# A decoder block on Trainium2: head 1's queries and keys as a Strassen pair, another order in a pair's second half, group norm's scaling on ScalarE

## The chip, the cores and the metric

The kernel runs on one core of one Trainium2 chip. The metric is the device time of one execution in microseconds (us). TensorE (PE) multiplies, VectorE (DVE) and ScalarE (ACT) work on tiles, GpSimd (POOL) does little arithmetic here and issues the accumulating DMAs, SyncE (SP) issues the plain ones. About 1% is what a measurement of this kernel can tell from no change.

## The reference

One layer of a hybrid decoder, batch 1, 512 tokens, 1024 channels, everything in float32: a chunkwise retention (4 heads, keys of 128, values of 256) beside a sliding-window attention with sinks (8 query heads, 2 key heads), then an MLP with squared ReLU.

```python
h = rmsnorm(x, pre_mix_norm)
q_r, k_r, v_r, g_r, q_s, k_s, v_s, gate_r, gate_s = split(h @ w_in)
ret = retention_chunkwise(q_r, k_r, v_r)         # (B, T, 4, 256)
    # per chunk of 128: o = (q k^T * decay) v + (q * decay) state
    # mu, var over the 256 channels of a head:  (o - mu) * rsqrt(var + EPS)
y_r = (silu(g_r) * ret) @ w_ret_out
y_s = swa_gqa_sinks(q_s, k_s, v_s, sinks) @ w_swa_out
merged = sigmoid(gate_r) * y_r + sigmoid(gate_s) * y_s
x = x + rmsnorm(merged @ w_out, post_mix_norm)
u = square(relu(rmsnorm(x, pre_mlp_norm) @ w_up))
x = x + rmsnorm(u @ w_down, post_mlp_norm)
```

The change touches the projection of `q_r` and `k_r` (how they are multiplied, not what) and the last line of the retention, the group norm of each head.

## The kernel before

Every float32 product is done as three matmuls of a reduced float32 type: an operand is split into a high part (a cast on ScalarE, line 144) and the rest (a subtraction on VectorE, line 145), and `mm3` multiplies high by high (L188), high by rest (L189, L190). So each weight tile that comes in as `raw` needs a cast to `whi` and a subtraction to `wlo` before TensorE can use it.

Many of the products are made with a Strassen scheme of one level (Winograd's form): instead of the eight products of half-size blocks there are seven. Of the tokens it needs the blocks `11`, `21`, `22` and four sums `t1` to `t4`, made once (`hB`; `hT` are the blocks and `hsum` the sums). Of the weights it needs the blocks `11`, `12`, `22` and four sums `s1` to `s4`. `sums_into` loads two blocks into a tile `rs` by a plain DMA on SP (L220) and adds two more by an accumulating DMA on POOL (L221), which has to wait until the plain one has landed; that gives `s1` and `s3`. `wino_weights` then works in this order: it splits `raw` into `11` and `12`, splits `rs` into `s1` and `s3` (`whi`, `wlo`), adds to `rs` in place twice on VectorE (L241, L242), which gives `s2` and `s4`, splits these into `p24`, and last splits `22` into `p22`.

The retention works head by head. In the loop over heads, head h computes its decayed keys, its scores, its state products (`ret_st`) and its values (`ret_v`), and between these stand the products that make the queries and keys of head h + 1. The constant `DIRECT` says how many heads are made by plain blocks. It is 2, so heads 0 and 1 are made by `ret_block` (24 matmuls of 128x512 each for queries and for keys, tile `pblk`), heads 2 and 3 by `ret_pair`: seven products of 12 matmuls of 128x256 (tiles `rpair`), four in `first()`, three in `second()`. One PSUM tile, `chain`, accumulates several of them, and ScalarE copies it out after each (L745 and others in `first()`, L753 in `second()`): the next product on `chain` can't start before that copy is done.

The sums of the weights of head 2 are loaded while the window heads are still at work, into a part of the tile `retn` that is not yet needed; those of head 3 are loaded into the pool `wx`, which is opened in head 0's turn after `bctx` has been closed. The place of that pool is free only when what lay there is done with, so its first load waits for the last matmul (`pso`) of the last window head, `swa_values(3)`. Behind it on SP come, in this order, the loads of `w_g` (the gate of the retention, `wide_sums`) and of the first sums of `w_gate`.

The order on each engine is the order of the program as a scheduler has arranged it; every engine works its list strictly in order and waits at its own instructions. The tile pools give a place again when the last reader has finished, and a load into it waits for that on its queue.

Group norm is done per head at the end of `ret_values`: `bns` and `mv` hold mean and variance, `rms` the variance plus a constant (VectorE), `rr` its power −1/2 (POOL), and four instructions on VectorE (L601), one for each block of 128 tokens, subtract the mean and multiply by `rr` from PSUM into `retn`. `retn` is read only after the stage.

Of the kernel before, what the change touches and what calls it, by code (L numbers as in the profile page):

```python
# [10 lines left out]
F32 = mybir.dt.float32  # L11
F32R = mybir.dt.float32r
AF = mybir.ActivationFunctionType
# [3 lines left out]
P = 128  # L17
# [17 lines left out]
WARM = 7  # L35
LEFT_AHEAD = 300
T2_DMA = 4
DIRECT = 2

C_QR, C_KR, C_VR, C_GR, C_QS, C_KS, C_GATE_R = (0, 512, 1024, 2048, 3072, 3584, 3840)  # L40

# [62 lines left out]
def block_kernel(ctx, tc, x, xT, pre_mix, w_in, w_qk, w_v, w_g, w_gate, w_ret, w_swa, w_out, sinks, post_mix,  # L104
# [119 lines left out]
    def wino_load(w):  # L224

        raw = raw_tile([P, 3, 4, P])
        nc.sync.dma_start(raw[:, 0:2], w[:, 2:4])
        nc.sync.dma_start(raw[:, 2], w[:, 0])
        return raw

    def wino_weights(wx, rs, raw, px=None):

        a11, a12, a22 = raw[:, 0], raw[:, 1], raw[:, 2]

        def two(t, i, j):
            return {i: tuple(a[:, 0] for a in t), j: tuple(a[:, 1] for a in t)}

        w = two(parts(raw[:, :2], [P, 2, 4, P]), "11", "12")
        yield w
        w.update(two(parts(rs, [P, 2, 4, P]), "s1", "s3"))  # L240
        nc.vector.tensor_tensor(rs[:, 0], rs[:, 0], a11, op=ALU.add)  # L241
        last["sum"] = nc.vector.tensor_tensor(rs[:, 1], rs[:, 0], a12, op=ALU.add)  # L242
        yield w
        p24 = [(px or wx).tile([P, 2, 4, P], F32R, name=f"p24{i}") for i in range(2)]
        split(p24[0], p24[1], rs)
        w.update(two(p24, "s2", "s4"))
        yield w
        with tc.issue_after(last["hi"].ins):
            p22 = [wx.tile([P, 4, P], F32R, name=f"p22{i}") for i in range(2)]
            split(p22[0], p22[1], a22)  # L250
        w["22"] = tuple(p22)
        yield w

    def wino_first(steps):
        return list(steps)[-1]
# [167 lines left out]
    nc.sync.dma_start(sink_sb, sinks.to_broadcast([P, SWA_HEADS]))  # L423


    def swa_queries(ps):

        qs = dpool.tile([P, SEQ], F32, name="qs", bufs=4)
        nc.vector.scalar_tensor_tensor(qs, ps, SWA_DH**-0.5, R, op0=ALU.mult, op1=ALU.mult)
        return qs  # L430

# [142 lines left out]
    def ret_values(q, pt, states, v, h):  # L574
        mv = rpool.tile([P, NT, 2], F32, name="mv")
        retn = retns[h // 2][:, :, (h % 2) * RET_DV : (h % 2 + 1) * RET_DV]
        pss = []
        for ip in range(2):
            ps = bank([P, 2, RET_DV], "ret_v")
            for i in range(2):  # L580
                c = 2 * ip + i
                mm3(
                    ps[:, i, :], tuple(a[:, c, :] for a in pt), tuple(a[:, c, :] for a in v),
                    True, c == 0,
                )
                if c:
                    mm3(
                        ps[:, i, :], tuple(a[:, (c - 1) * P : c * P] for a in q),
                        states[c - 1], False, True,
                    )  # L590
            for i in range(2):
                st = rpool.tile([P, nc.vector.BN_STATS_DIM], F32, name="bns")
                nc.vector.bn_stats(st, ps[:, i, :])
                nc.vector.bn_aggr(mv[:, 2 * ip + i, :], st)
            pss.append(ps)
        ms = rpool.tile([P, NT], F32, name="rms")
        r = rpool.tile([P, NT], F32, name="rr")
        nc.vector.tensor_scalar(ms, mv[:, :, 1], chunk_sb[:, 1, h : h + 1], None, op0=ALU.add)
        nc.gpsimd.tensor_tensor(r, ms, mhalf, op=ALU.pow)
        for ib in range(NT):  # L600
            nc.vector.tensor_scalar(  # L601
                retn[:, ib, :], pss[ib // 2][:, ib % 2, :], mv[:, ib, 0:1], r[:, ib : ib + 1],
                op0=ALU.subtract, op1=ALU.mult,
            )


# [78 lines left out]

    def load_qk(h):
        if h >= DIRECT:
            return wino_first(wino_weights(wx, qk_sums[h], wino_load(w_qk[h - DIRECT])))
        return load_feature_blocks(w_in, (C_QR + h * RET_DK, C_KR + h * RET_DK))


    qs = [swa_queries(qs_ps[0])]
    kk2 = dpool.tile([P, SWA_KV, NT, 2, SWA_DH], F32, name="kk2", tag="s")
    ksT = dpool.tile([P, SWA_KV, SEQ], F32, name="ksT", bufs=1)
    for g in range(SWA_KV):
        for i in range(2):
            nc.gpsimd.tensor_copy(kk2[:, g, :, i, :], kv[:, :, g * SWA_DH : (g + 1) * SWA_DH])
    qs.append(swa_queries(qs_ps[1]))
    wq = load_feature_pair(w_in, C_QS + 256)
    qs.append(swa_queries(project_block(wq[0], xg)))  # L700
    for g in range(SWA_KV):
        ps = bank([P, SEQ])
        for t in range(NT):
# [4 lines left out]
    sv = wide_sums(accpool, w_v, tag="acc")  # L708
    for k in range(KD):
        norm_input(k)  # L710
    qs.append(swa_queries(project_block(wq[1], xg)))
    wqk = load_qk(0)
    xgctx.close()
    vpool = sctx.enter_context(tc.tile_pool(name="vpool", bufs=1, side="right"))
# [18 lines left out]
    def ret_pair(a, b):  # L733

        qk = [rpool.tile([P, SEQ], F32, name="qk", tag="qk") for _ in range(2)]
        out = [t[:, i * 256 : (i + 1) * 256] for t in qk for i in range(2)]
        chain, p25, p3 = bank([P, 256], "rpair"), bank([P, 2, 256], "rpair"), bank([P, 256], "rpair")

        def first():
            wino_product(chain, a["11"], b["11"])  # L740
            nc.scalar.copy(out[0], chain)
            wino_product(p25[:, 0], a["12"], b["21"])
            nc.vector.tensor_tensor(out[0], p25[:, 0], out[0], op=ALU.add)
            wino_product(chain, a["s2"], b["t2"], False)
            nc.scalar.copy(out[1], chain)  # L745
            wino_product(p3, a["s4"], b["22"])
            nc.vector.tensor_tensor(out[1], p3, out[1], op=ALU.add)

        def second():
            wino_product(p25[:, 1], a["s1"], b["t1"])  # L750
            nc.vector.tensor_tensor(out[1], p25[:, 1], out[1], op=ALU.add)
            wino_product(chain, a["s3"], b["t3"], False)
            nc.scalar.mul(out[3], chain, -1.0)  # L753
            nc.vector.tensor_tensor(out[3], out[3], p25[:, 1], op=ALU.subtract)
            wino_product(chain, a["22"], b["t4"], False)
            nc.scalar.mul(out[2], chain, -1.0)

        return first, second, qk
# [14 lines left out]
    for i in range(3):  # L773
        next(steps)
        probs_t = swa_transpose(probs)
        probs = swa_scores(i + 1, qs[i + 1])
        next(steps)
        if i == 2:
            wqk = load_qk(1)
        swa_values(i, probs_t)  # L780
    retn_all = accpool.tile([P, 2, NT, 512], F32, name="retn", tag="acc")
    retns = [retn_all[:, i] for i in range(2)]
    qk_sums = {
        DIRECT: sums_into(
            retn_all[:, 1, 0:2].rearrange("p t (k c) -> p t k c", c=P), w_qk[0]
        )
    }

    for h in range(RET_HEADS):
        if 0 < h < RET_HEADS - 1:  # L790
# [19 lines left out]
        if h == 0:  # L810
            swa_values(3, probs_t)

            bctx.close()
            gctx = ExitStack()
            wx = wino_pool(gctx)
            pad(wx, 64)
            qk_sums[DIRECT + 1] = wino_sums(wx, w_qk[1])
            xyctx = ExitStack()
            xypool = xyctx.enter_context(tc.tile_pool(name="xypool", bufs=1))
        if h + 1 >= RET_HEADS:  # L820
# [601 lines left out]
```

## Time and profile before

| | before |
|---|---|
| median of 3 timed runs | 726.5 us (726.38 to 733.58) |
| profiled execution | 722.91 us |
| its span | 721.1 us, mean granted clock 0.995 |
| TensorE busy | 706.7 us, 98% of the span |
| VectorE, ScalarE, GpSimd busy | 543.6, 424.7, 62.3 us |
| DMA | 119.37 MB, mean 166 GB/s |

The profile is of one execution, by the hardware's own profiler. A row of its timeline gives start and duration in us, the engine, the line of the kernel, the operation, and the tile written and those read; in brackets stands how long the engine had been idle and what ended that. A row of the waits gives the engine, its tile and line, what it waited for, and then the total in us, the number of times and the longest. A row of the windows gives, for each stretch of time, the busy us of TensorE, its weight loads, VectorE, ScalarE and GpSimd, and then the granted clock, the share of the DMA engines and GB/s. A row of a DMA issue gives the queue, the size and the time from issue to landing. SPq and POOLq mean the sequencer of the engine, which issues.

### The profile page before, as it was taken

To read this page: it belongs to the slowest core of one execution; us is meant where nothing else is said; L and a number is where in the kernel's file an instruction comes from. 1 tells how busy PE (TensorE), PEld (TensorE's weight loads), DVE (VectorE), ACT (ScalarE), POOL (GpSimd) and SP (SyncE) were. 2 spreads that over 40 slices of the span, in tenths; PEclk is the share of its full clock that TensorE was granted. 3 is DMA by queue.
4 is the path that set the end of the run, shared out by engine and by line. 5 is a ranking of instruction groups with operands and counts; after the bars stand their busy time and mean duration, and the time that the engine had idled before them with its cause. 6 is when DMAs were issued, how large, how long until landed. Compare 5 with 4: busy or idle time off the path is not lost.

```text
span 721.1 us, 11428 instructions
## 1 busy us (share of the span) xinstructions
PE 706.7 (98%) x4510; PEld 631.6 (88%) x4510; DVE 543.6 (75%) x824; ACT 424.7 (59%) x720; POOL 62.3 (9%) x77
## 2 busy tenths in 40 slices
PE   8999999999999999999999999999999999999996
PEld 8877878998888989999888999999999788888885
DVE  4599988798885667666845876777776788987797
ACT  5657866455565535244643776666768656655571
POOL 0300000111100000000002100000000110010010
PEclk9999999999999999999999999999999999999999
DMA  9955522966434365462563517777853999698603
GB/s 299 324 173 104 117 74 74 299 169 116 108 128 139 102 169 146 117 192 73 188 279 117 148 57 229 209 194 192 204 158 119 303 277 237 150 206 197 117 1 116
DMA packets 40597, 119.37 MB, mean 166 GB/s; under 512 B 3552, under 2 KB 16992, under 8 KB 34400
## 3 DMA queue, kind: packets, MB, share of 16 engines
q1 hardware_dynamic: 33488, 81.28, 32.0%
q0 software_dynamic: 6768, 37.23, 28.0%
q8 instruction: 35, 0.57, 0.3%
q10 hardware_dynamic: 288, 0.14, 0.1%
q14 instruction: 18, 0.15, 0.1%
HBM read 116.54 MB, written 2.10 MB: 165 GB/s over the span
## 4 chain that ended last, share of the span: by engine, by line
PE 76%; DVE 10%; ACT 5%; DMA 5%; issue 2%; SPq 1%; POOL 0%; DVEq 0%; POOLq 0%; ACTq 0%
PE wino L188 9%; PE wino L190 9%; PE wino L189 9%; PE p L190 5%; PE p L189 5%; PE p L188 5%; DVE wlo L145 3%; PE wide L188 3%; PE wide L190 3%; PE wide L189 3%; PE ps L189 2%; PE ps L190 2%; PE yr L190 2%; PE yr L188 2%; PE yr L189 2%
## 5 line engine op out<-in xcount | busy, mean ns | idle before, releaser
L145 DVE TENSOR_TENSOR wlo<-raw,whi 128x1024 fp32r<-128x1024 f32 x79 | 96.1, 1222 | 43.0 <-ACT whi L144 42.9
L144 ACT CAST whi<-raw 128x1024 fp32r<-128x1024 f32 x79 | 82.7, 1052 | 38.5 <-DMA raw<-in_w_in 8.7
L190 PE MATMUL p<-whi,left 128*128 128x512 f32 x216 | 84.1, 390 | 0.2 <-DVE left L145 0.2
L189 PE MATMUL p<-wlo,left 128*128 128x512 f32 x216 | 84.2, 390 | 0.0
L188 PE MATMUL p<-whi,left 128*128 128x512 f32 x216 | 84.0, 390 | 0.1
L190 PEld LDWEIGHTS p<-whi,left 128*128 128x128 f32 x216 | 40.5, 188 | 9.3 <-DVE left L145 1.0
L189 PEld LDWEIGHTS p<-wlo,left 128*128 128x128 f32 x216 | 40.5, 188 | 9.0 <-DVE wlo L145 0.5
L188 PEld LDWEIGHTS p<-whi,left 128*128 128x128 f32 x216 | 40.5, 188 | 8.7 <-ACT left L144 0.5
L145 DVE TENSOR_TENSOR wlo<-tch,whi 128x1024 fp32r<-128x1024 f32 x32 | 38.6, 1218 | 8.0 <-ACT whi L144 8.0
L144 ACT CAST p<-rs 128x1024 fp32r<-128x1024 f32 x22 | 23.1, 1051 | 35.4 <-DVE rs L242 35.3
L144 ACT CAST left<-uc 128x1024 fp32r<-128x1024 f32 x28 | 29.3, 1051 | 22.3 <-PE p L189 22.3
L145 DVE TENSOR_TENSOR left<-uc,left 128x1024 fp32r<-128x1024 f32 x28 | 34.1, 1219 | 9.5 <-ACT left L144 9.5
L144 ACT CAST whi<-tch 128x1024 fp32r<-128x1024 f32 x32 | 33.2, 1050 | 12.4 <-PE p L190 6.8
L145 DVE TENSOR_TENSOR p<-rs,p 128x1024 fp32r<-128x1024 f32 x22 | 27.0, 1225 | 15.1 <-ACT p L144 15.0
L145 DVE TENSOR_TENSOR wlo<-rs,whi 128x1024 fp32r<-128x1024 f32 x22 | 26.9, 1223 | 11.5 <-ACT whi L144 9.1
L188 PE MATMUL wino<-h2s,p 128*128 128x256 f32 x104 | 28.7, 276 | 0.0
L189 PE MATMUL wino<-h2s,p 128*128 128x256 f32 x104 | 28.7, 276 | 0.0
L190 PE MATMUL wino<-h2s,p 128*128 128x256 f32 x104 | 28.7, 276 | 0.0
L188 PE MATMUL wino<-h2c,whi 128*128 128x256 f32 x104 | 28.7, 276 | 0.0
L189 PE MATMUL wino<-h2c,whi 128*128 128x256 f32 x104 | 28.7, 276 | 0.0
L190 PE MATMUL wino<-h2c,wlo 128*128 128x256 f32 x104 | 28.7, 276 | 0.0
L188 PE MATMUL wino<-h2s,whi 128*128 128x256 f32 x104 | 28.7, 276 | 0.0
(394 smaller groups left out, 2355.4 us busy)
## 6 DMA issues: line engine op xcount, KB each, us to landing
tch<-in_w_down POOLq DMA_DIRECT2D x12, 1024.0 KB, 8.8
raw<-in_w_down SPq DMA_DIRECT2D x7, 1024.0 KB, 7.1
rs<-in_w_up SPq DMA_DIRECT2D x13, 512.0 KB, 4.2
rs<-in_w_up POOLq DMA_DIRECT2D x13, 512.0 KB, 5.5
raw<-in_w_up SPq DMA_DIRECT2D x13, 512.0 KB, 5.2
acc<-in_w_v POOLq DMA_DIRECT2D x4, 1024.0 KB, 8.0
rs<-in_w_gate SPq DMA_DIRECT2D x8, 512.0 KB, 3.8
acc<-in_w_g POOLq DMA_DIRECT2D x4, 1024.0 KB, 8.0
```

The lines of the kernel that those rows point to most:

```text
L144: last["hi"] = nc.scalar.copy(hi, src)
L145: last["split"] = nc.vector.tensor_tensor(lo, src, f(hi), op=ALU.subtract)
L188: nc.tensor.matmul(ps, ah, bh, start=first, stop=False, skip_group_check=more)
L189: nc.tensor.matmul(ps, ah, bl, start=False, stop=False, skip_group_check=more)
L190: nc.tensor.matmul(ps, al, bh, start=False, stop=last, skip_group_check=more)
```

## The change

There are three edits. `DIRECT` becomes 1: head 1 is made by a pair as well, and its weights come from `w_qk`, which now holds heads 1 to 3. Its sums lie in a tile that takes a place of the window queries (these are now made two to a tile), its `p24` and `p22` in a tile `early_qk` of another pool, and both are loaded within the loop of the window heads. Head 2's sums no longer go to `retn`: they are loaded with those of head 3 into `wx`, after `bctx` has been closed. The second edit swaps two products in `second()`. The third replaces the four VectorE instructions of group norm by four activations on ScalarE, with `rr` as the scale and a small new tile `shift` (minus mean times `rr`, one VectorE instruction for the four blocks) as the bias.

```diff
-DIRECT = 2
+DIRECT = 1
...
+        p24 = places[0] if places else [
+            (px or wx).tile([P, 2, 4, P], F32R, name=f"p24{i}") for i in range(2)
+        ]
...
         r = rpool.tile([P, NT], F32, name="rr")
         nc.vector.tensor_scalar(ms, mv[:, :, 1], chunk_sb[:, 1, h : h + 1], None, op0=ALU.add)
         nc.gpsimd.tensor_tensor(r, ms, mhalf, op=ALU.pow)
+        shift = rpool.tile([P, NT], F32, name="shift")
+        nc.vector.scalar_tensor_tensor(
+            shift, mv[:, :, 0], -1.0, r, op0=ALU.mult, op1=ALU.mult
+        )
         for ib in range(NT):
-            nc.vector.tensor_scalar(
-                retn[:, ib, :], pss[ib // 2][:, ib % 2, :], mv[:, ib, 0:1], r[:, ib : ib + 1],
-                op0=ALU.subtract, op1=ALU.mult,
+            nc.scalar.activation(
+                retn[:, ib, :], pss[ib // 2][:, ib % 2, :], AF.Identity,
+                bias=shift[:, ib : ib + 1], scale=r[:, ib : ib + 1],
             )
...
         if h >= DIRECT:
-            return wino_first(wino_weights(wx, qk_sums[h], wino_load(w_qk[h - DIRECT])))
+            return wino_first(wino_weights(
+                wx if h > 1 else None, qk_sums[h], wino_load(w_qk[h - DIRECT]), places=qk_places.get(h)
+            ))
...
         def second():
+            wino_product(chain, a["s3"], b["t3"], False)
+            nc.scalar.mul(out[3], chain, -1.0)
             wino_product(p25[:, 1], a["s1"], b["t1"])
             nc.vector.tensor_tensor(out[1], p25[:, 1], out[1], op=ALU.add)
-            wino_product(chain, a["s3"], b["t3"], False)
-            nc.scalar.mul(out[3], chain, -1.0)
             nc.vector.tensor_tensor(out[3], out[3], p25[:, 1], op=ALU.subtract)
             wino_product(chain, a["22"], b["t4"], False)
...
         next(steps)
+        if i == 1:
+            rs = dpool.tile([P, 2, 4, P], F32, name="rs1", tag="qs")
+            qk_sums = {1: sums_into(rs, w_qk[0])}
         if i == 2:
+            early_qk = accpool.tile([P, 6, 4, P], F32R, name="early_qk", tag="acc")
+            qk_places = {
+                1: ([early_qk[:, i : i + 2] for i in (0, 2)], [early_qk[:, i] for i in (4, 5)])
+            }
             wqk = load_qk(1)
         swa_values(i, probs_t)
     retn_all = accpool.tile([P, 2, NT, 512], F32, name="retn", tag="acc")
     retns = [retn_all[:, i] for i in range(2)]
-    qk_sums = {
-        DIRECT: sums_into(
-            retn_all[:, 1, 0:2].rearrange("p t (k c) -> p t k c", c=P), w_qk[0]
-        )
-    }
...
             pad(wx, 64)
-            qk_sums[DIRECT + 1] = wino_sums(wx, w_qk[1])
+            for i in (2, 3):
+                qk_sums[i] = wino_sums(wx, w_qk[i - DIRECT])
```

How this moves the instructions is seen on three engines. The first place is SP's list around the loads for the retention's queries and keys. Before, `retn_1222` is the load of head 2's sums, `rs_1355` that of head 3's, `acc` and the last `raw` are of `w_g`:

```order
L168 DMA raw_1194<-in_w_in 128x8x128 x2
L227 DMA raw_1436<-in_w_qk 128x1024
L228 DMA raw_1436<-in_w_qk 128x512
L220 DMA retn_1222<-in_w_qk 128x1024
L227 DMA raw_1655<-in_w_qk 128x1024
L228 DMA raw_1655<-in_w_qk 128x512
L220 DMA rs_1355<-in_w_qk 128x1024
L618 DMA acc_1879<-in_w_g 128x2048
L620 DMA acc_1879<-in_w_g 128x2048
L611 DMA raw_2053<-in_w_g 128x2048
```

After, `rs1` is head 1's sums, `rs_1391` head 2's, `rs_1394` head 3's, and the three `raw` those of heads 1, 2 and 3:

```order
L227 DMA raw_1196<-in_w_qk 128x1024
L228 DMA raw_1196<-in_w_qk 128x512
L220 DMA rs1_1022<-in_w_qk 128x1024
L227 DMA raw_1490<-in_w_qk 128x1024
L228 DMA raw_1490<-in_w_qk 128x512
L227 DMA raw_1711<-in_w_qk 128x1024
L228 DMA raw_1711<-in_w_qk 128x512
L220 DMA rs_1391<-in_w_qk 128x1024
L220 DMA rs_1394<-in_w_qk 128x1024
L630 DMA acc_1937<-in_w_g 128x2048
L632 DMA acc_1937<-in_w_g 128x2048
L220 DMA rs_2518<-in_w_gate 128x1024
```

The load of head 2's sums has moved behind head 3's raw weights, to the place where the first load into `wx` stands, and the last `raw` load of `w_g` has moved behind the first sums of `w_gate` (`rs_2518`).

The second place is ScalarE's list at the end of head 0's turn, where head 2's weights are prepared. Before, head 2's sums need only their second split here (`p240_1449`, from `retn_1222`), and `whi_1658` is of head 3:

```order
L144 CAST swaT_624<-pso_1331 128x512
L144 CAST st0_1325<-st_1327 128x256
L144 CAST p240_1449<-retn_1222 128x1024
L144 CAST p220_1453<-raw_1436 128x512
L144 CAST whi_1457<-vg_591 128x1024
L724 COPY qk_1361<-pblk_1362 128x512
L144 CAST whi_1658<-raw_1655 128x1024
L144 CAST qc0_1432<-qk_1248 128x384
```

After, `whi_1497` is the first split of head 2's sums, `p240_1503` the second; `whi_1511` is of head 1's values, `kd0` of its keys, `whi_1714` and `whi_1718` of head 3's weights and sums:

```order
L144 CAST swaT_622<-pso_1367 128x512
L765 ACTIVATE qk_1255<-rpair_1256 128x256
L770 ACTIVATE qk_1255<-rpair_1256 128x256
L144 CAST qc0_1486<-qk_1254 128x384
L144 CAST whi_1497<-rs_1391 128x1024
L144 CAST whi_1511<-vg_589 128x1024
L543 ACTIVATE kd0_1519<-ret_k_1515,chunk_sb_529 128x384
L144 CAST whi_1714<-raw_1711 128x1024
L144 CAST whi_1718<-rs_1394 128x1024
L144 CAST p240_1503<-rs_1391 128x1024
L613 ACTIVATE retn_1230<-ret_v_1441,shift_1480,rr_1477 128x256 x2
L613 ACTIVATE retn_1230<-ret_v_1457,shift_1480,rr_1477 128x256 x2
```

Both splits of head 2's sums now stand behind head 1's finished pair, and the first split of head 3's sums stands between them; group norm's scaling of head 0 follows.

The third place is TensorE's list in head 1's turn, at the first matmuls from `p24` in head 2's pair. Before:

```order
L190 MATMUL rpair_1483<-hT0_84,wlo_1440 128x256
L188 MATMUL rpair_1483<-hT0_84,whi_1439 128x256
L189 MATMUL rpair_1483<-hT1_85,whi_1439 128x256
L190 MATMUL rpair_1483<-hT0_84,wlo_1440 128x256
L188 MATMUL rpair_1482<-hsum0_86,p240_1449 128x256
L189 MATMUL rpair_1482<-hsum1_87,p240_1449 128x256
```

After, `ret_st` are the state products of head 1:

```order
L190 MATMUL rpair_1537<-hT0_84,wlo_1494 128x256
L188 MATMUL rpair_1538<-hT0_84,p240_1503 128x256
L189 MATMUL rpair_1538<-hT1_85,p240_1503 128x256
L188 MATMUL ret_st_1591<-whi_1511,kd0_1519 128x256
L189 MATMUL ret_st_1591<-wlo_1512,kd0_1519 128x256
L190 MATMUL ret_st_1591<-whi_1511,kd1_1520 128x256
```

The first matmuls from `p24` still stand directly behind the products of `11` and `12`, now those of `s4`·`22` in place of `s2`·`t2`, and the state products have moved in between them and the rest.

More of the change, by code (lines that the diff above doesn't have):

```diff
@@ L229, in wino_load, with wino_weights @@
         return raw
-    def wino_weights(wx, rs, raw, px=None):
+    def wino_weights(wx, rs, raw, px=None, places=None):
         a11, a12, a22 = raw[:, 0], raw[:, 1], raw[:, 2]
@@ L243, in wino_weights @@
         yield w
-        p24 = [(px or wx).tile([P, 2, 4, P], F32R, name=f"p24{i}") for i in range(2)]
+        p24 = places[0] if places else [
+            (px or wx).tile([P, 2, 4, P], F32R, name=f"p24{i}") for i in range(2)
+        ]
         split(p24[0], p24[1], rs)
@@ L248, in wino_weights @@
         with tc.issue_after(last["hi"].ins):
-            p22 = [wx.tile([P, 4, P], F32R, name=f"p22{i}") for i in range(2)]
+            p22 = places[1] if places else [
+                wx.tile([P, 4, P], F32R, name=f"p22{i}") for i in range(2)
+            ]
             split(p22[0], p22[1], a22)
@@ L423, in block_kernel, with swa_queries @@
     nc.sync.dma_start(sink_sb, sinks.to_broadcast([P, SWA_HEADS]))
-    def swa_queries(ps):
-        qs = dpool.tile([P, SEQ], F32, name="qs", bufs=4)
+    q_tiles = []
+    def swa_queries(i, ps):
+        if i % 2 == 0:
+            q_tiles.append(dpool.tile([P, 2, SEQ], F32, name="qs", tag="qs"))
+        qs = q_tiles[-1][:, i % 2]
         nc.vector.scalar_tensor_tensor(qs, ps, SWA_DH**-0.5, R, op0=ALU.mult, op1=ALU.mult)
@@ L687, in load_qk @@
         if h >= DIRECT:
-            return wino_first(wino_weights(wx, qk_sums[h], wino_load(w_qk[h - DIRECT])))
+            return wino_first(wino_weights(
+                wx if h > 1 else None, qk_sums[h], wino_load(w_qk[h - DIRECT]), places=qk_places.get(h)
+            ))
         return load_feature_blocks(w_in, (C_QR + h * RET_DK, C_KR + h * RET_DK))
-    qs = [swa_queries(qs_ps[0])]
+    qs = [swa_queries(0, qs_ps[0])]
     kk2 = dpool.tile([P, SWA_KV, NT, 2, SWA_DH], F32, name="kk2", tag="s")
@@ L697, in block_kernel @@
             nc.gpsimd.tensor_copy(kk2[:, g, :, i, :], kv[:, :, g * SWA_DH : (g + 1) * SWA_DH])
-    qs.append(swa_queries(qs_ps[1]))
+    qs.append(swa_queries(1, qs_ps[1]))
     wq = load_feature_pair(w_in, C_QS + 256)
-    qs.append(swa_queries(project_block(wq[0], xg)))
+    qs.append(swa_queries(2, project_block(wq[0], xg)))
     for g in range(SWA_KV):
@@ L710, in block_kernel @@
         norm_input(k)
-    qs.append(swa_queries(project_block(wq[1], xg)))
+    qs.append(swa_queries(3, project_block(wq[1], xg)))
     wqk = load_qk(0)
```

## The prediction

> **What bounds the kernel now.** I read the page first (its head, its first part and the chain of part 4).
>
> ```profile
> span 721.1 us, 11428 instructions
> PE 706.7 (98%) x4510; PEld 631.6 (88%) x4510; DVE 543.6 (75%) x824; ACT 424.7 (59%) x720; POOL 62.3 (9%) x77
> ...
> PE 76%; DVE 10%; ACT 5%; DMA 5%; issue 2%; SPq 1%; POOL 0%; DVEq 0%; POOLq 0%; ACTq 0%
> ```
>
> TensorE is busy for 706.7 of 721.1 us and carries 76% of the chain that ended last. So a matmul less shortens the run only while everything feeds TensorE in time, and any new wait of TensorE is added whole. The second view is the waits of TensorE between 100 and 200 us, the retention stage, where the change lies.
>
> ```profile
> PE rpair L188 <- ACT qk L753: 1.4, 2, 1.1
> ```
>
> There are two stalls in that stage, 1.4 us together, the longer 1.1; both wait for ScalarE's copy of `chain` to be finished before `22`·`t4` accumulates on it. The third view is TensorE's timeline through the places that the change touches (start, duration, line, tile).
>
> ```profile
> 115.37 0.48 PE L188 MATMUL pblk<-hT,whi 128*128 128x512 f32 x1
> ...
> 121.05 0.49 PE L496 MATMUL psd<-ident,s 128*128 128x128 f32 x3
> ...
> 125.83 0.50 PE L188 MATMUL pblk<-hT,whi 128*128 128x512 f32 x1
> ...
> 131.54 0.28 PE L188 MATMUL ret_v<-whi,pt 128*128 128x256 f32 x1
> ...
> 135.19 0.37 PE L188 MATMUL rpair<-hT,whi 128*128 128x256 f32 x1
> ...
> 138.01 0.28 PE L188 MATMUL rpair<-hsum,p 128*128 128x256 f32 x1
> ...
> 140.73 0.28 PE L188 MATMUL ret_st<-whi,kd 128*128 128x256 f32 x1
> ...
> 145.71 0.28 PE L189 MATMUL ret_v<-wlo,pt 128*128 128x256 f32 x1
> 147.08 0.38 PE L188 MATMUL rpair<-hsum,p 128*128 128x256 f32 x1 [1.09 <-ACT qk L753]
> ```
>
> Head 1's query block runs from 115.37 to 121.05 and its key block from 125.83 to 131.54. Head 2's pair starts at 135.19, and at 138.01 it needs its first weights made from the sums (`p24`); its first half ends at 140.73.
>
> **Head 1 as a pair: −1.7.** The two blocks took 5.68 + 5.71 = 11.39 us. A pair's first half (48 matmuls) took 140.73 − 135.19 = 5.54; the second half has 36 such matmuls, three quarters of that, 4.16. The difference is 11.39 − 9.70 = −1.69 us. The casts of the weights grow, but ScalarE is 59% busy and no stall for them is in the view of waits; head 1's sums are fetched in the window loop, long ahead of 115, so I take them at nothing. If they were late, the same preparation as below would show there.
>
> **The other order of a pair's second half: −1.7.** With `s1`·`t1` (12 matmuls, 1.4 us) between `s3`·`t3` and `22`·`t4`, the copy has time. From 145.71 to 147.08 is 1.37 us where matmuls of this shape follow each other at 0.115 (5.54/48), so 1.25 us go; the smaller stall (1.4 − 1.1 = 0.3 us idle) carries the same 0.15 on top of its idle time, so 0.44. The sum is −1.69. What is late next there is the copy of the last product, which nobody on TensorE waits for at once.
>
> **Head 2's sums come late: +8.1.** Before, they were loaded in the `retn` tile during the window heads, and only head 3's went through `wx` once `bctx` had closed. Now `retn` is no longer lent, and head 2's load takes the place that head 3's had on SP: behind the last `pso` matmul of `swa_values(3)`. The timelines of SP and POOL and what the issues tell of the landing show what that place is worth.
>
> ```profile
> 126.04 0.33 SPq L220 DMA_DIRECT2D rs<-in_w_qk  x1
> 126.42 0.43 SPq L618 DMA_DIRECT2D acc<-in_w_g  x1
> 126.89 1.23 SPq L620 DMA_DIRECT2D acc<-in_w_g  x1
> 129.67 0.33 SPq L611 DMA_DIRECT2D raw<-in_w_g  x1
> 130.04 0.44 SPq L220 DMA_DIRECT2D rs<-in_w_gate  x1
> ...
> 130.65 0.87 POOL L221 DMA_DIRECT2D rs<-in_w_qk  x1 [22.36 <-DMA rs<-in_w_qk]
> 133.69 0.88 POOL L619 DMA_DIRECT2D acc<-in_w_g  x1 [2.17 <-DMA acc<-in_w_g]
> ```
>
> ```profile
> rs<-in_w_qk SPq DMA_DIRECT2D x1, 512.0 KB, 3.9
> ...
> rs<-in_w_qk POOLq DMA_DIRECT2D x1, 512.0 KB, 10.4
> ...
> retn<-in_w_qk POOLq DMA_DIRECT2D x1, 512.0 KB, 5.4
> ...
> rs<-in_w_up POOLq DMA_DIRECT2D x1, 512.0 KB, 7.9
> ...
> raw<-in_w_qk SPq DMA_DIRECT2D x1, 512.0 KB, 3.2
> ...
> acc<-in_w_g POOLq DMA_DIRECT2D x1, 1024.0 KB, 13.9
> ```
>
> The load goes out at 126.04, less the 0.14 by which half a pair (5.54) is shorter than a block (5.68): 125.9. It lands 3.9 later, 129.8, and POOL issues the accumulate 0.7 after that, as before (126.04 + 3.9 = 129.94, issued 130.65): 130.5. How long it takes is not known. The row of the same place took 10.4 us, beside four transfers of `w_g` and `w_gate`; the row of head 2's own accumulate on quiet queues 5.4; one in the MLP, beside two loads, 7.9. In the new order 1.5 MB of those neighbours (the rows at 129.67 and 130.04) wait for tiles that head 2's casts free later, and head 3's 0.5 MB are in front instead. Some, but not all, of the crowd is left, so I take 7.9, with 5.4 and 10.4 as bounds: landed at 138.4.
>
> From there a chain of casts has to run before the first `p24` matmul; the chain of waits shows it in the gate stage, where it runs bare.
>
> ```profile
> 238.07 0.96 ACT whi L144
> 239.03 0.02 issue
> 239.06 1.22 DVE wlo L145
> 240.28 0.34 DVE sgr L293
> 240.62 0.61 DVE rs L241
> 241.22 0.02 issue
> 241.25 0.70 DVE rs L242
> ...
> 242.03 1.06 ACT p L144
> ```
>
> That is 243.09 − 238.07 = 5.02 us, less the foreign 0.34 (`sgr`): 4.68. In the new order VectorE also has group norm's small step and `wlo<-vg` between L241 and L242, one more 128x1024 subtraction at 1.22 and about 0.1: 6.0 us. Head 2's first `p24` matmul can so start at 138.4 + 6.0 = 144.4. TensorE is ready for it at 138.01 − 1.69 = 136.3. The wait is 8.1 us; with 5.4 it is 5.6, with 10.4 it is 10.6. Queued behind it on TensorE is all the rest, in order: head 1's state products, its values, head 2's scores. Nothing else on TensorE stands in front that could fill the gap.
>
> What else queues behind late sums: on SP the raw load of `w_g` and the `w_gate` sums move from 130 to about 147. No wait of TensorE in the view above is for `w_g`, whose third product, in head 3's stage, reads that tile; I take the load as still covered, and a new wait there would be its price if it is not. On POOL head 0's `rr` stands behind `w_g`'s accumulate, on ScalarE the scaling behind `p24`; both serve only `retn`, read after the stage.
>
> **The clock after a wait: +1.6.** The windows of 2 us around TensorE's first long wait show the granted clock in the third column from the right.
>
> ```profile
> 6.00:8.00 2.00, 1.86 (x12) 1.67 (x13) 2.00 (x6) 1.48 (x3) 0.00 (x0) 0.90 0.97 288
> 8.00:10.00 2.00, 2.00 (x12) 2.00 (x11) 0.85 (x2) 0.94 (x2) 0.00 (x0) 0.50 1.06 364
> 10.00:12.00 2.00, 2.00 (x15) 2.00 (x15) 1.78 (x4) 1.94 (x5) 0.00 (x0) 0.75 0.89 273
> ```
>
> After sparse work the clock was 0.50 for all of 8 to 10 us and for parts of its neighbours: (1 − 0.90)·2 + (1 − 0.50)·2 + (1 − 0.75)·2 = 1.7 us of full speed lost, of which I take 1.6 for the matmuls that would have filled it. A wait of 8 us should bring one such spell. Its bounds are 0 (no drop) and 3.2 (two spells). The Trainium skill's page "TensorE: Matmul & The Clock Gate", section "Part 1: The HAM clock gate", says that an idle window of about 3.4 us halves the clock until a busy window has passed; the 0.50 row agrees, and the rule speaks against this change, since by it a wait of 8 us can't go without the drop.
>
> **Group norm on ScalarE: 0.** The rows of line L601 (VectorE, count and min/median/max ns) and L753 (a ScalarE pass of the same shape) price it.
>
> ```profile
> L601 DVE TENSOR_SCALAR retn<-ret_v,mv,rr x16: 531/535/544, 137.9 to 190.2; 128x256 f32<-128x256 f32 x16
> ...
> L753 ACT ACTIVATE qk<-rpair x2: 370/372/375, 146.6 to 161.7; 128x256 f32<-128x256 f32 x2
> ```
>
> VectorE loses 16 × 0.535 = 8.6 us, ScalarE gains 16 × 0.372 = 6.0. Neither bounds the stage. Head 0's four stand behind the `p24` cast and in front of `22` and `pt`; 4 × 0.372 = 1.5 us there could cost TensorE 0.3 if the rest is tight, or save as much where VectorE's splits come sooner. I take 0 ± 0.3.
>
> **The sum.** −1.69 − 1.69 + 8.1 + 1.6 = +6.3. The profiled execution took 722.91 us (span 721.1 and 1.8 around it), so it should become 729.2. The three timed runs have a median of 726.5 (726.38 to 733.58), 3.6 above it; I add the same 6.3 to the median: 732.8.
>
> **Rivals.**
>
> *Quiet queues.* Head 2's accumulate takes 5.4, the row of `retn`. For it: half the neighbours have left. Against it: 2 MB of `w_g` go out on SP right behind the load, and 10.4 was measured there. The wait is 5.6: −3.38 + 5.6 + 1.6 = +3.8, 730.3. Chance 0.18.
>
> *Head 3's sums hold head 2 up: slower.* On ScalarE the cast of head 3's sums now stands in front of head 2's `p24` cast. It doesn't matter while head 3's accumulate lands less than 3.9 us behind head 2's (6.0, less 1.06 for each of the two casts). It goes out about 0.9 later, after the 0.87 of the first; at 10.4 it would land at 141.8, 3.4 behind, just in time; at the 13.9 of the row of `w_g` beside it at 145.3, and the two casts end at 147.4. The wait is 11.1: −3.38 + 11.1 + 1.6 = +9.3, 735.8. Chance 0.18.
>
> *The accumulate costs no more than a plain load.* The lowest row of 512 KB is 3.2: landed 133.7, weights 139.7, a wait of 3.4, so 0 without a drop of the clock and +1.6 with it, 726.5 to 728.1. Against it speak all three accumulate rows. Chance 0.05. The Trainium skill's page "DMA: Bandwidth & Descriptors", section "Anatomy of one DMA — SWDGE (gpsimd) path", fits 2.0 us and bytes by 436 GB/s, which also gives 3.2 for 512 KB; the accumulates of this trace differ from it.
>
> *The weights are there in time.* Then the edits pay as summed: −3.4, 723.1. It needs a landing by 130.3, when before the load itself had only just landed. Chance 0.07, for an error of mine in which instruction SP waits for.
>
> **How the numbers follow.** The forecast has the remaining 0.52, with its own range from 730.3 (the quiet bound) to 735.3 (10.4 us, a wait of 10.6). The range from 726.0 to 737.0 takes in every case but the weights in time and the far end of the bounds, where 10.4 and two spells of the clock meet (−3.38 + 10.6 + 3.2 = +10.4, 736.9). About 1%, 7.3 us, is what a measurement of this kernel can tell from no change. Slower by over that: the third case and three tenths of the forecast's, 0.18 + 0.16 = 0.34. Faster by over that needs twice what the edits can give: 0.03. The rest, 0.63, is within.
>
> **What would show it.** Right: a wait of TensorE of some 8 us ahead of the first `rpair` matmul from `p24` in head 2's pair, released by the `p24` cast, a granted clock of 0.5 behind it, no wait on the `chain` copy, and 9.7 us of `rpair` in head 1. Wrong: the load of head 2's sums issued well before 125 us, or its accumulate landed by 131; a long wait of TensorE in head 1's or head 3's pair; or ScalarE as the releaser of anything through group norm's scaling.

## The result

The changed kernel takes 737.59 us (median of 20 runs, 731.97 to 746.22), the kernel before in the same sessions 726.59 (20 runs, 720.95 to 734.1). The ratio is 1.0134, with an interval from 1.0111 to 1.0156: slower by 9.7 us (8.1 to 11.3). The prediction had +6.3 us, 732.8, with a range to 737.0; the median lies 0.6 above that range, the ratio times 726.5 (736.2) inside it. Direction and mechanism were those forecast, the size was 3.4 us short, and "within 1%", which had a chance of 0.63, did not come; "slower by over 1%" had 0.34.

The profiled execution took 731.97 us. The head of its page, as before:

```profile
span 730.2 us, 11512 instructions
...
PE 708.4 (97%) x4546; PEld 635.0 (87%) x4546; DVE 541.6 (74%) x820; ACT 433.4 (59%) x740; POOL 62.3 (9%) x78
...
PE 85%; DVE 6%; DMA 4%; ACT 3%; issue 2%; POOL 0%; POOLq 0%; DVEq 0%; SPq 0%; ACTq 0%
```

TensorE is busy 1.7 us longer, the span 9.1. So TensorE waits, and the view of its waits between 100 and 200 us says where:

```profile
PE rpair L188 <- ACT p L144: 9.2, 1, 9.2
PE ret_v L188 <- ACT pt L144: 1.0, 1, 1.0
PE wide L188 <- ACT vg L676: 0.4, 1, 0.4
```

Before, there were two waits of 1.4 us together in this view, both for the `chain` copy. They are gone, and one of 9.2 for the `p24` cast stands there, with 1.0 for the `pt` cast (the decayed scores) behind it. The rows of SP, POOL, ScalarE and TensorE that lead to it, and the issue's time to landing:

```profile
122.23 0.80 SPq L220 DMA_DIRECT2D rs<-in_w_qk  x2
123.09 0.42 SPq L630 DMA_DIRECT2D acc<-in_w_g  x1
123.55 0.43 SPq L632 DMA_DIRECT2D acc<-in_w_g  x1
```

```profile
126.08 0.87 POOL L221 DMA_DIRECT2D rs<-in_w_qk  x1 [48.02 <-DVE qk L768]
128.31 0.87 POOL L221 DMA_DIRECT2D rs<-in_w_qk  x1 [1.35 <-DMA rs<-in_w_qk]
```

```profile
rs<-in_w_qk POOLq DMA_DIRECT2D x1, 512.0 KB, 10.2
```

```profile
136.28 1.04 ACT L144 CAST whi<-rs 128x1024 fp32r<-128x1024 f32 x1 [6.80 <-DMA rs<-in_w_qk]
...
139.59 1.04 ACT L144 CAST whi<-rs 128x1024 fp32r<-128x1024 f32 x1
141.09 1.04 ACT L144 CAST p<-rs 128x1024 fp32r<-128x1024 f32 x1 [0.46 <-DVE rs L242]
```

```profile
142.19 0.58 PE L188 MATMUL rpair<-hT,p 128*128 128x256 f32 x1 [9.16 <-ACT p L144]
...
162.31 0.39 PE L188 MATMUL ret_v<-whi,pt 128*128 128x256 f32 x1 [0.98 <-ACT pt L144]
```

The load of head 2's sums goes out at 122.23, the accumulate at 126.08, and it lands at 136.28 after 10.2 us. The first matmul from `p24` starts at 142.19, 5.9 us later. The clock behind the wait, in the windows of 2 us (third column from the right):

```profile
142.00:144.00 2.00, 1.81 (x8) 1.82 (x9) 2.00 (x3) 2.00 (x6) 0.00 (x0) 0.50 0.17 33
144.00:146.00 2.00, 2.00 (x12) 2.00 (x11) 2.00 (x4) 1.94 (x5) 0.00 (x0) 0.50 0.77 258
146.00:148.00 2.00, 2.00 (x18) 2.00 (x18) 1.93 (x4) 0.00 (x0) 0.70 (x1) 0.94 0.85 225
```

That is 0.5·1.81 + 0.5·2 + 0.06·2 = 2.0 us of full speed lost.

The time from one landmark of TensorE's timeline to the next shows each part by itself. The landmarks are the transposes of the keys (`ret_k`) with which each head's turn begins, the first product of `w_g` (`wide`, just behind head 3's) and the first product of the gates (`wino`). All in us; the last column is where head 0's turn begins. Head 3's 1.1 us of its own is left out, since it is the same in all.

| kernel | head 0's turn | head 1's | head 2's | `w_g` to the gates | begins at |
|---|---|---|---|---|---|
| before | 19.88 | 15.69 | 15.00 | 67.44 | 114.17 |
| changed | 18.16 | 25.93 | 15.77 | 68.95 | 110.73 |
| e1: sums early | 18.17 | 19.78 | 14.71 | 68.89 | 112.01 |
| e2: late sums alone | 19.47 | 27.88 | 16.62 | 67.43 | 110.78 |
| e3: order alone | 19.88 | 16.20 | 14.79 | 67.44 | 113.17 |
| e4: norm back on VectorE | 17.98 | 26.77 | 16.42 | 68.37 | 112.99 |
| e5: busy wait | 18.10 | 29.39 | 14.52 | 68.92 | 111.15 |
| e6: quiet queues | 18.13 | 22.83 | 14.46 | 71.50 | 112.58 |
| e7: query pairs alone | 19.87 | 15.96 | 15.00 | 67.43 | 119.38 |
| e8: norm alone | 19.87 | 16.82 | 14.68 | 68.78 | 119.06 |
| e9: order, `w_g` held | 19.88 | 16.29 | 15.99 | 67.42 | 112.26 |
| e10: early, `w_g` held | 18.17 | 18.94 | 14.69 | 69.75 | 112.13 |
| e11: same, norm on VectorE | 18.25 | 18.97 | 15.42 | 68.13 | 111.05 |
| e12: busy wait in order | 18.15 | 26.47 | 14.56 | 68.89 | 112.19 |

### The profile page after: what moved, and what is told of

Read it like the earlier page. It is cut to its first block, busy times and chain, and to the rows that moved or that the text cites. A ratio compares the mean times of both kernels' runs of the same rounds, so it can differ in the third digit from the quotient of the medians.

```text
span 730.2 us, 11512 instructions
## 1 busy us (share of the span) xinstructions
PE 708.4 (97%) x4546; PEld 635.0 (87%) x4546; DVE 541.6 (74%) x820; ACT 433.4 (59%) x740; POOL 62.3 (9%) x78
## 4 chain that ended last, share of the span: by engine, by line
PE 85%; DVE 6%; DMA 4%; ACT 3%; issue 2%; POOL 0%; POOLq 0%; DVEq 0%; SPq 0%; ACTq 0%
PE wino L188 9%; PE wino L190 8%; PE wino L189 8%; PE p L190 5%; PE p L189 5%; PE p L188 5%; PE wide L188 3%; PE wide L189 3%; PE wide L190 3%; DVE wlo L145 2%; PE yr L189 2%; PE ps L188 2%; PE ps L190 2%; PE yr L188 2%; PE yr L190 2%; PE ps L189 2%
## 5 line engine op out<-in xcount | busy, mean ns | idle before, releaser
L145 DVE TENSOR_TENSOR wlo<-rs,whi 128x1024 fp32r<-128x1024 f32 x24 | 29.4, 1223 | 19.1 <-ACT whi L144 16.1
L144 ACT CAST whi<-tch 128x1024 fp32r<-128x1024 f32 x32 | 33.2, 1050 | 11.3 <-PE p L190 6.7
L144 ACT CAST whi<-rs 128x1024 fp32r<-128x1024 f32 x24 | 25.3, 1054 | 10.1 <-DMA rs<-in_w_qk 6.8
```

The source lines that it names most:

```text
L144: last["hi"] = nc.scalar.copy(hi, src)
L145: last["split"] = nc.vector.tensor_tensor(lo, src, f(hi), op=ALU.subtract)
```

## The experiments

**e1, head 2's sums early.** The sums go to the place of the second pair of window queries, and `p24` to tiles of the stream, so that both are done before the pool is closed:

```diff
         if i == 2:
+            rs2 = dpool.tile([P, 2, 4, P], F32, name="rs2", tag="qs")
+            qk_sums[2] = sums_into(rs2, w_qk[1])
...
+            ahead = wino_weights(None, qk_sums[2], wino_load(w_qk[1]), places=late_places)
+            for _ in range(3):
+                next(ahead)
             bctx.close()
```

> The changed kernel with one thing moved: head 2's sums are loaded in the window loop, into the place of the second pair of window queries, and split before that pool is closed. Theory (the late sums are the loss): the wait of 9.2 us for the p24 cast, the half clock behind it (some 3 us) and the 1.0 us for pt go; against the changed kernel -12 to -14 us, so 0.3 to 0.8% below the kernel before. Rival (the loss is in the rest of the change, the clock or crowded queues whatever the place of the load): it stays at least 0.5% above the kernel before, with waits elsewhere in the stage.

It took 730.41 us, 1.0089 of the kernel before (1.0055 to 1.0122). The wait of 9.2 and the half clock are gone, and head 1's turn is 6.2 us shorter than in the changed kernel. Over all four stretches of the table e1 is 7.3 us shorter than the changed kernel and 3.5 longer than the kernel before. So by the stretches the late sums are the larger part of the loss; but the theory that they are all of it fell, and the rival was right in so far. The timed runs give the edit less: by the two ratios some 3.3 us, about 3 either way, and why is open. What is left are waits of TensorE that were not there before:

```profile
PE rpair L188 <- ACT qk L765: 2.5, 1, 2.5
PE rpair L188 <- ACT qk L755: 1.5, 1, 1.5
```

ScalarE's timeline of e1 shows why L765 is late:

```profile
144.62 1.04 ACT L144 CAST whi<-rs 128x1024 fp32r<-128x1024 f32 x1 [3.91 <-DMA rs<-in_w_qk]
145.57 0.38 ACT L765 ACTIVATE qk<-rpair 128x256 f32<-128x256 f32 x1
```

This is the copy that the new order of `second()` was to hide. It is not the number of matmuls behind it that sets its time: it stands on ScalarE behind the cast of head 3's sums, and that cast waits for a DMA. L755 is the copy behind `11`·`11`; it stands behind head 0's four scalings and the `pt` cast.

**e2, the late sums alone.** The kernel before with only this edit:

```diff
-    qk_sums = {DIRECT: sums_into(retn_all[:, 1, 0:2]..., w_qk[0])}
+    qk_sums = {}
...
-            qk_sums[DIRECT + 1] = wino_sums(wx, w_qk[1])
+            for i in (2, 3):
+                qk_sums[i] = wino_sums(wx, w_qk[i - DIRECT])
```

> The kernel before with one thing done: head 2's sums go into wx after bctx is closed, as in the change; heads 0 and 1 stay direct blocks, the order and group norm stay. Theory: load out at 126, accumulate about 10 us, landed at 141, first p24 matmul near 147 where TensorE was ready at 138: a wait of 8 to 9.5 us and some 3 us of half clock, so 1.4 to 1.8% slower than before. By the prediction's price of 7.9 for the accumulate: a wait of about 7, and 1.1% slower with 1.6 for the clock. Rival (another part of the change makes the loss): under 0.5% slower.

Measured: 736.9 us, 1.0181 (1.0136 to 1.0226), which is 13 us, a little over the theory's upper end. The view of its waits shows the same long wait, and two for the rest of the split:

```profile
PE rpair L188 <- ACT p L144: 7.9, 1, 7.9
PE rpair L190 <- DVE p L145: 2.0, 2, 1.4
```

This one edit makes the whole slowdown and 3 us more, of which the pair of head 1 wins 1.7 back. The clock is part of it: here it stayed at 0.50 to 150 us and cost 3.9 us by the sum used above, against 2.0. The rival is out. One thing more can be read from this view: the order of `second()` is the old one, and yet no wait for a `chain` copy is left.

**e3, the order alone.** The swap of the two products in `second()`, in the kernel before.

> The kernel before with only the other order in a pair's second half. Theory: the two waits for the chain copy go, -1.7 us, 0.2% faster, and no wait of TensorE takes their place. Rival: the copy is not the only thing late there (the next wait comes up at once), no change.

No change: 1.0001 (0.9967 to 1.0036). In the stretches, head 1's and head 2's turns are 30.99 us together, before 30.69. The two waits are gone, and the rival was right:

```profile
PE rpair L188 <- ACT qk L745: 1.8, 2, 1.6
```

```profile
141.19 1.04 ACT L144 CAST whi<-rs 128x1024 fp32r<-128x1024 f32 x1 [4.25 <-DMA rs<-in_w_qk]
142.14 0.36 ACT L745 COPY qk<-rpair 128x256 f32<-128x256 f32 x1
```

L745 is the copy behind `s2`·`t2`, in `first()`. The next product on `chain` is `s3`·`t3`, and by the swap it comes 12 matmuls sooner: `s1`·`t1`, which now covers the copy L753, had covered L745. And L745 is late because ScalarE stood in front of it in the cast of head 3's sums, which waited for their accumulate until 141.19 (in the kernel before they landed at about the same time, 130.65 + 10.4 = 141.05).

**e4, group norm's scaling back on VectorE,** in the changed kernel (the four lines of L601 before).

> The changed kernel with group norm's scaling back on VectorE. Theory: the four scalings stood in front of the pt cast on ScalarE, so the wait of 1.0 us for pt behind the long wait goes, and no other takes its place: -1 us, 0.1% below the changed kernel, 1.2% above the kernel before. Rival: VectorE's p24 and pt subtractions come later by what the scaling takes there (4 x 0.53), and the time stays or grows by 1 us.

740.35 us, 1.0222 (1.0175 to 1.027), against 1.0134 of the changed kernel. The wait for `pt` is gone and the stretch behind `w_g`'s first product 0.6 shorter, but the rival's point holds too:

```profile
PE rpair L188 <- ACT p L144: 9.3, 1, 9.3
PE rpair L190 <- DVE p L145: 1.4, 1, 1.4
```

Head 1's and head 2's turns together are 1.5 us longer than in the changed kernel. By the two ratios this kernel is some 6 us (0.9%) slower than the changed one; its profile shows 0.7 of that between the start of head 0's turn and the gates, and the rest stays open.

**e5 and e12, TensorE kept busy.** Sixty matmuls whose result is overwritten, ahead of the first matmul from `p24`; in e12 the product `s4`·`22` is also written in front of `s2`·`t2`:

```diff
+            if h == 1:
+                for _ in range(60):
+                    nc.tensor.matmul(p3, a["11"][0][:, 0], b["11"][0][:, 0], start=True, stop=True)
+                wino_product(p3, a["s4"], b["22"])
             wino_product(chain, a["s2"], b["t2"], False)
```

> The changed kernel with 60 extra matmuls (128x256, their result overwritten) on TensorE ahead of head 2's first matmul from p24, so that TensorE works for 6.9 us of its wait. Theory: the wait has its length from the sums, so it ends at the same time, and the clock stays at 1.0 behind it: 2 to 3.5 us below the changed kernel (the prediction's term was 1.6). Rival (the clock costs nothing, since the casts behind the wait set the pace): no change.

> The changed kernel with 60 extra matmuls of 128x256 (6.9 us, overwritten) ahead of head 2's first matmul from p24, with s4 by 22 kept as the first product from p24, so that no copy of chain stands in the way. Theory: the wait shrinks to some 2 us and ends where it did, the granted clock stays 1.0 behind it, and head 1's turn is 1.5 to 2.5 us shorter than the 25.9 us of the changed kernel. Rival: the clock falls all the same, or the turn has the same length since the casts behind set the pace.

e5 took 736.14 us (1.0166, 1.0108 to 1.0224) and answered nothing: with `s2`·`t2` first, TensorE waited 5.4 us for the copy L755 (behind `11`·`11`, on the same tile `chain`), which ScalarE had behind the `p24` cast and the scalings, and head 1's turn became 29.39. In e12 (737.46, 1.0145, 1.0103 to 1.0187) the long wait shrank as meant, yet head 1's turn stayed, at 26.47:

```profile
PE rpair L188 <- ACT p L144: 2.3, 1, 2.3
...
PE rpair L190 <- DVE p L145: 0.8, 1, 0.8
```

```profile
142.00:144.00 2.00, 0.40 (x2) 0.30 (x2) 2.00 (x5) 1.50 (x3) 0.00 (x0) 1.00 0.87 180
144.00:146.00 2.00, 1.24 (x8) 1.14 (x8) 2.00 (x3) 2.00 (x6) 0.00 (x0) 0.84 0.12 29
146.00:148.00 2.00, 2.00 (x11) 1.94 (x11) 1.89 (x4) 1.63 (x3) 0.00 (x0) 0.50 0.94 287
```

The clock fell all the same, some 2 us after the longer wait had ended. So the rival was right: the long idle time is not needed for the drop, and what the clock costs here could not be taken away by filling 6.9 of 9.2 us.

**e6, quiet queues.** GpSimd writes a few elements of `w_g`'s tile, read from head 2's sums, so that `w_g`'s two loads wait for the accumulate:

```diff
+            g_sums = xypool.tile([P, 2, 4, 512], F32, name="acc")
+            for i in range(2):
+                nc.gpsimd.tensor_copy(g_sums[:, i, 0, 0:4], qk_sums[2][:, 0, 0, 0:4])
```

> The changed kernel with w_g's two loads held back until head 2's accumulate has landed (GpSimd writes a few of their elements after it). Theory (neighbours make the accumulate slow): it takes 5.4 to 6.5 us instead of 10.2, and the first split of head 2's sums starts 4 to 5 us earlier against the load's issue. The scheduler has put the four scalings in front of the p24 cast in this kernel, so that the time falls by only 1 to 3 us. Rival (an accumulate at this place takes 10 whatever runs beside it): no change in the landing.

```profile
127.68 0.87 POOL L221 DMA_DIRECT2D rs<-in_w_qk  x1 [47.71 <-DVE qk L768]
...
133.16 0.31 POOL L840 COPY acc<-rs 128x4 f32<-128x4 f32 x2 [3.40 <-DMA rs<-in_w_qk]
```

```profile
rs<-in_w_qk POOLq DMA_DIRECT2D x1, 512.0 KB, 5.4
```

Without the 2 MB of `w_g` beside it the accumulate takes 5.4 us, the price that head 2's had on quiet queues before; the theory holds. The wait of TensorE falls to 5.5 us and head 1's turn by 3.1. With two runs the time (1.0106, 1.0 to 1.0213) says little, and a new wait of 1.9 us behind `w_g`'s first product takes part of it back.

**e7, the window queries two to a tile,** in the kernel before, and **e8, group norm's scaling on ScalarE alone.**

> The kernel before with only the window queries made two to a tile. TensorE reached the retention stage 3.4 us sooner in the changed kernel, mostly since two waits of query blocks for wlo (1.8 us) between 18 and 56 us were gone. Theory (the places and so the order of the casts changed with these tiles): the two waits go here as well, -1 to -3 us. Rival (they went since head 1's blocks are no longer loaded there, or by chance of one execution): the waits stay, no change.

> The kernel before with only group norm's scaling on ScalarE. Theory: 0 to +1 us, no wait over 0.5 us by it. Rival: ScalarE's list in the stage becomes late as in the changed kernel (pt 1.0 us) at each head, +2 to +4 us.

e7: 1.0004 (0.9961 to 1.0048). e8: 0.9997 (0.9955 to 1.0039). Their profiled executions (735.59 and 735.55) are longer than all their other runs, so only stretches are read from them, and e8's also against e7's. In the profiles of both there is a wait of the first stage, longer than before, which by e7's theory should have gone (e8's is 5.5):

```profile
PE pblk L190 <- DVE wlo L145: 5.6, 1, 5.6
```

So e7's theory fell. e3 and e9 change nothing ahead of the retention stage; it began there at 113.17 and 112.26, with 0.4 us of this wait and none, against 114.17. In e2, too, TensorE's list is that of the kernel before down to the transposes of the last window head, and its retention stage began at 110.78 with no such wait. This wait was 0, 0.4, 1.8 (in two) and 5.6 us in executions of the same work: it is scatter, and so, at least in the main, is the 3.4 us head start of the changed kernel's profile.

In e8 the stretch from `w_g`'s first product to the gates is 68.78, against 67.43 in e7 and 67.44 before. ScalarE's timeline there:

```profile
195.44 1.94 ACT L605 ACTIVATE retn<-ret_v,shift,rr 128x256 f32<-128x256 f32 x4 [1.56 <-DVE shift L601]
197.26 0.60 ACT L668 COPY vg<-wide 128x512 f32<-128x512 f32 x1
```

The four scalings first wait 1.56 us for `shift` and then take 1.9, and the copy of a product of `w_g` that TensorE waits for (0.3 us, and 0.3 for a `wlo` 2 us later) comes behind them. That is +1.3 us where 0 was forecast. The copy L757 behind `s3`·`t3` is later as well (a wait of 2.1 us, in e7 1.6 in two), and over all four stretches e8 is 1.9 us longer than e7 and 2.1 than the kernel before. So the theory's "0 to +1" is missed, and the lower end of the rival's +2 to +4 is near; in the whole time (−0.2 us, −3.3 to +2.8) it is too small to be seen.

**e9, the order with `w_g` held back** until head 3's accumulate has landed (e6's edit, in the kernel before, with `qk_sums[3]`), **e10,** the same in e1, and **e11,** with the scaling on VectorE as well.

> The kernel before with the other order in a pair's second half and with w_g's two loads held back until head 3's accumulate has landed. With the order alone a wait of 1.6 us for the chain copy L745 came in place of those removed, because ScalarE stood in front of that copy in the cast of head 3's sums, which landed at 141.2. Theory: the accumulate lands 4 to 5 us earlier, the cast is out of the way, and all waits for chain copies go: head 1's turn to the first product of w_g 1.7 us shorter than before, 0.2% faster. Rival (the copy is late for another reason, as the matmuls of two products are too short to cover it): a wait of over 1 us stays at L745 or L753.

> The changed kernel with head 2's sums early, and w_g's loads held back until head 3's accumulate has landed. Theory: the wait of 2.5 us for the copy L765, behind the cast of head 3's sums, goes; that of 1.5 for L755, behind the four scalings, stays, and so does the 1.4 us that the stretch from w_g's first product to the gates has lost since the scaling is on ScalarE: 0.3 to 0.6% above the kernel before. Rival: the wait for L765 stays.

> As the last, and group norm's scaling back on VectorE. Theory (the scaling on ScalarE costs 1.5 us in head 1's turn and 1.4 us behind w_g's first product): no wait over 0.5 us between 110 and 235, the retention stage 3 us shorter than before, the stretch from w_g's first product to the gates 67.4 as before: 0.3 to 0.6% faster than the kernel before. Rival: VectorE, with 8.6 us more, is late with a subtraction (1.4 us, as in the changed kernel with the scaling on VectorE): no change against before.

e9: 1.0022 (0.9995 to 1.005). The accumulate still took 8.5 us; the sums of `w_gate` and a load of `w_g` (`raw`) had moved into the gap. The wait of e3 in head 1's turn, for the copy behind `s2`·`t2`, went as the theory had it. But one of 0.9 came there for the copy behind `s3`·`t3` (L752 in that kernel), and one of 1.4 in head 2's turn for the copy behind `s2`·`t2` (L746). By its letter that is the rival; its reason, products too short to cover a copy, is not what the rows show. Both times ScalarE stood in front of the copy in a cast that waited for VectorE, 3.53 us for `st` and 1.66 for `pt`.

e10: 1.0033 (1.0003 to 1.0063), as expected; the wait for L765 went, that for L755 (L756 in that kernel) stayed at 1.5. Not expected were a wait of 0.9 for `kd`, a clock of 0.89, 0.50 and 0.76 from 138 to 144 us, and a stretch behind `w_g`'s first product 2.3 us longer than before instead of 1.4.

e11: 1.0041 (1.0015 to 1.0067) where 0.3 to 0.6% faster was expected: the rival again, with VectorE late and the clock down once more (L752 is here the copy behind `11`·`11`).

```profile
PE ret_st L188 <- DVE retn L609: 1.4, 2, 1.0
...
PE rpair L188 <- ACT qk L752: 0.5, 1, 0.5
```

```profile
134.00:136.00 2.00, 1.16 (x10) 0.95 (x9) 0.89 (x2) 0.74 (x2) 1.98 (x2) 1.00 0.68 242
136.00:138.00 2.00, 1.30 (x6) 0.90 (x7) 2.00 (x5) 0.00 (x0) 0.00 (x0) 1.00 0.99 270
138.00:140.00 2.00, 2.00 (x14) 2.00 (x14) 1.90 (x6) 1.50 (x4) 0.00 (x0) 0.64 1.02 203
140.00:142.00 2.00, 2.00 (x11) 2.00 (x11) 1.67 (x3) 1.06 (x2) 1.08 (x2) 0.51 1.06 211
```

None of the versions tried beats the kernel before.

## Why the prediction was right, and where its sizes were off

**Head 1 as a pair: right.** −1.69 forecast; head 0's turn is 18.16 against 19.88, −1.72, and 18.0 to 18.3 in every kernel with the pair.

**Head 2's sums come late: right in kind, one term too small.** The cause is shown, by e2 (doing it alone gives the loss) and e1 (undoing it alone takes the wait away). From the load's issue to the first `p24` matmul I had 18.5 us; it was 142.19 − 122.23 = 20.0. The landing of the load and the issue of the accumulate came at 3.85 (4.6 forecast), the chain of casts took 5.9 (6.0), and the accumulate 10.2, where I took 7.9 between the bounds 5.4 and 10.4. The step that failed is the reason for 7.9: that with 1.5 MB of the neighbours held back some of the crowd is gone. e6 shows that `w_g`'s 2 MB are the crowd. The nearest row was the one of the same place, 10.4, and it should have been the value. The wait was 9.2 instead of 8.1.

**The clock: right, a little short.** 2.0 us against 1.6. But that the length of the wait makes the drop, as the rule weighed there has it, is not what e12, e11 and e1 show (last section). Nor did the row that I called agreeing with it: it has the 0.50, but the longest wait of TensorE ahead of it was 1.4 us.

```profile
5.96 0.38 PE L188 MATMUL ptok<-wkv,xg 128*128 128x256 f32 x1 [1.44 <-ACT wkv L144]
```

**The other order: wrong as an edit by itself.** I had −1.69 and wrote that what is late next is the copy of the last product, for which nobody waits at once. That step failed: `s3`·`t3` itself needs a copy of `chain`, the one behind `s2`·`t2`, and lost its cover. e3 shows that wait at 1.6 us, and no gain. I had also read only who released TensorE (a copy), and not what held ScalarE: in e3 a cast that waited for a DMA, and at the wait that I wanted to remove, in the kernel before, two casts in front of the copy, the first of which had waited for VectorE:

```profile
145.39 0.41 ACT L144 CAST st<-st 128x256 fp32r<-128x256 f32 x1 [1.73 <-DVE st L566]
145.70 1.04 ACT L144 CAST whi<-vg 128x1024 fp32r<-128x1024 f32 x1
146.65 0.38 ACT L753 ACTIVATE qk<-rpair 128x256 f32<-128x256 f32 x1
```

In the changed kernel the waits for `chain` copies are gone, and 9.16 + 2.0 − 1.25 = 9.9 is near the 10.24 by which head 1's turn grew. But that is not the swap's merit: in e2, with the late sums and the old order, no such wait is left either. So no run shows a gain from the order, and that the sum could keep this term is luck.

**Group norm on ScalarE: a term put too low.** 0 ± 0.3 forecast. In the changed kernel TensorE waits 0.98 us for `pt`, whose cast came behind the four scalings:

```profile
159.84 1.92 ACT L613 ACTIVATE retn<-ret_v,shift,rr 128x256 f32<-128x256 f32 x4
161.64 0.62 ACT L144 CAST pt<-pt 128x512 fp32r<-128x512 f32 x1
```

And the stretch from `w_g`'s first product to the gates grew by 1.5, with e8 showing 1.3 for the edit alone. I had priced the engine's load (59% busy) and one place in its list; what counts is what stands behind the four instructions at each of the four heads. That it is a cost of its own in the changed kernel is read from the trace, not shown by a run: taking the scaling back there (e4) shortens the stretch behind `w_g`'s first product by 0.6 and removes the wait for `pt`, but VectorE is then late, and the four stretches together grow by 0.7. Over the four stretches the edit costs 2.1 us in the kernel before (e8) and 0.8 in e10 against e11.

**The sum by what was measured.** −1.72 (pair) + 10.24 (head 1's turn) + 0.77 (head 2's) + 1.51 (`w_g`) = +10.8 from the start of head 0's turn to the gates; the timed runs have +9.7 (8.1 to 11.3). Against the +6.3, the wait and the clock gave 1.5 more; the wait for `pt` and the longer stretch behind `w_g`'s first product, where the scaling stands, 2.5; 0.5 is left open. All these misses are on one side.

**The rivals.** Quiet queues (5.4) came true only where e6 made the queues quiet. Head 3's sums did not hold head 2 up: in the rows of the result their cast follows at 139.59 with no wait of its own, and `p24` waited 0.46 for VectorE. The plain-load price and the weights in time are out.

**The signs.** The signs for right came, with a wait of 9.2 for 8. Two of those for wrong came by their letter. The load went out at 122.23, before 125, but only because the stage began earlier: that is 11.5 us into head 0's turn, where 11.7 was forecast. And ScalarE released TensorE late through group norm's scaling, at `pt`; that one is the error named above.

## What to carry to other kernels

A wait that ends at a copy is not the copy's: before an edit is credited with it, look at what the copying engine did just ahead, since in an in-order list a cast that waits for a DMA or for VectorE holds everything behind it. When a transfer is moved to a place where another stood, take the price of the transfer that stood there, and ask who else loads at that moment. And where scaling or copying is moved to an engine with time to spare, go through its list at each place and name what comes behind.

## What was not expected of the hardware

**The clock falls after short waits too.** In e11 TensorE was busy for 2.46 of the 4 us from 134 to 138, with waits of 1.0 and 0.4 us, and had a clock of 0.64 and 0.51 in the next 4, a loss of 1.7 us. In e1 it waited for 2.5 us in one piece and was busy for only 1.54 of the 4 us from 142 to 146, and no drop followed:

```profile
142.00:144.00 2.00, 1.54 (x14) 1.35 (x12) 0.38 (x2) 0.00 (x0) 0.00 (x0) 1.00 1.06 260
144.00:146.00 2.00, 0.00 (x1) 0.00 (x1) 0.30 (x1) 1.38 (x3) 0.00 (x0) 1.00 1.07 264
146.00:148.00 2.00, 2.00 (x17) 2.00 (x18) 2.00 (x5) 1.51 (x3) 0.00 (x0) 1.00 0.99 238
```

So neither the longest wait nor the busy share of such a stretch tells by itself whether a drop comes. The Trainium skill's page "TensorE: Matmul & The Clock Gate", section "Part 1: The HAM clock gate", ties the drop to an idle window of about 3.4 us; e11's waits were shorter and the drop came. The runs here don't settle what decides.

**The same matmuls at the same granted clock ran at two paces.** The windows from 460 to 540 us, in the MLP, where TensorE never waits, of the kernel before and of e3:

```profile
460.00:540.00 80.00, 80.00 (x708) 80.00 (x708) 60.32 (x78) 55.10 (x101) 6.96 (x8) 1.00 0.75 192
```

```profile
460.00:540.00 80.00, 80.00 (x682) 80.00 (x681) 58.71 (x76) 53.59 (x99) 6.96 (x8) 1.00 0.71 185
```

708 matmuls in 80 us and 682, both at a clock of 1.00. The profiles of the changed kernel, e2 and e10 have 709, 709 and 708, those of all other runs 681 or 682. From the first `wino` matmul of the MLP to the first of the last product (`p`) it is 122.4 against 127.2 us, about as much as lies between the two groups into which most timed runs of the kernel before fall, at 720 to 723 and at 725 to 731. e3's own timed runs lie in both groups (719.8 to 720.6 and 724.8 to 728.6), so it seems to depend on the execution and not on the edit; each kernel has one profile, so no trace shows one kernel at both paces. Whole spans of two profiles can't be set against each other here, only stretches, and whole times only over many runs. Its cause stays open.
